# Summing the last two blocks of a prefix-sum kernel on VectorE with two input streams and an accumulator

## The chip, the cores and the metric

One core of a Trainium2 chip. The metric is the device time of one execution in microseconds (us); most executions of a kernel agree within 0.3%. The engines are named as in the profile: PE = TensorE, DVE = VectorE, ACT = ScalarE, POOL = GpSimd, SP = SyncE.

## The reference

```python
B, H, W = 4, 4224, 4224          # x: float32, 285 MB
ps = np.cumsum(np.cumsum(x, axis=1), axis=2)
diag = np.diagonal(ps, axis1=1, axis2=2)
return np.cumsum(diag, axis=1).astype(np.float32)
```

Output i of a batch is a cumulative sum, along the diagonal, of the sums of all x[r, c] with r and c up to i. So every element is read once, and what counts is a sum for each row (left of the diagonal) and for each column (above it).

## The kernel before

The input streams through three strip buffers; GpSimd issues the loads, which convert float32 to bf16. ScalarE and VectorE sum rows, TensorE sums columns. What follows is the end of the last batch, the only part that the change touches. The last 128 rows come as four blocks of 32 rows, each laid out as 128 partitions (4 per row) of 1024 columns. Blocks 0 and half of 1 are folded on TensorE, the rest are summed.

```python
def act_sum(acc, src):                      # ScalarE: copy with accumulator
    w = src.shape[-1]
    dump = dumpool.tile([P, 2176], BF16, name="dump")
    nc.scalar.activation(out=dump[:, :w], in_=src, func=ACT.Copy, accum_out=acc)

def row_sums(acc, src):                     # VectorE: reduction
    nc.vector.reduce_sum(out=acc, in_=src, axis=AX.X)
# ... (the stream, parts of the tail)
bcut = 640                                  # block 3 is loaded in two pieces
for sb, c0, c1 in ((0, 0, CB), (1, 0, CB), (2, 0, CB), (3, 0, bcut), (3, bcut, CB)):
    nc.gpsimd.dma_start(out=part_b[:, sb, c0:c1], in_=...)
# ...
act_sum(bsum[:, 0:1], part_b[:, 1, c1a:])
nc.scalar.copy(out=by, in_=by_ps)
weigh(arows[:, 0:1], weights, 0, fins[:1], start=True)   # fp32 matmuls, [128,1] x [128,n]
weigh(arows[:, 1:2], weights, P, fins[:1])
# ... (arows, dtot, bsum 0 and ones_col into fin_m and fin_e)
finish(fin_a, 0, M0)                        # VectorE: yl = fin + c12
act_sum(bsum[:, 1:2], part_b[:, 2, : CB // 2])
row_sums(bsum[:, 2:3], part_b[:, 2, CB // 2 :])
for k in (1, 2):
    weigh(bsum[:, k : k + 1], weights4, M0 + 2 * R, fins)
esum = last.tile([P, 4], FP32, name="esum")
for k, (c0, cm, c1) in enumerate(((0, 320, bcut), (bcut, bcut + 128, CB))):
    act_sum(esum[:, 2 * k : 2 * k + 1], part_b[:, 3, c0:cm])
    row_sums(esum[:, 2 * k + 1 : 2 * k + 2], part_b[:, 3, cm:c1])
for k in range(4):
    weigh(esum[:, k : k + 1], weights4, E0, fins)
finish(fin_m, M0, E0)
# ... store of 352 values, finish(fin_e), store of 32 values
```

## Time and profile before

| | us |
|---|---|
| time, median of the first 3 runs | 670.04 (669.3 to 670.96) |
| time, median of 6 runs with those of the comparison | 669.36 (668.34 to 670.96) |
| span of the profiled execution | 666.5 |
| landing of block 1, block 2, block 3 first piece, final piece | 660.83, 662.12, 662.91, 663.38 |
| final add (VectorE's addition of the last 32 values) | 664.36 |
| final add behind the final landing | 0.97 |

The landings are from the trace's semaphore records: the time at which the last of the 16 DMA engines reports. I call the last row the gap. (The prediction has 0.98 for it, from rounded times.) The prediction shows the profile lines.

### The profile page before, as it was taken

The numbers are of one execution on the slowest core, as the hardware profiler recorded it, in microseconds if no ns is written. First come the engines' busy times: TensorE is split into PE (matmuls) and PEld (weight loads), VectorE is DVE, ScalarE is ACT, GpSimd is POOL, SyncE is SP. The second block draws the span as 40 slices with busy tenths as digits, with TensorE's granted clock in tenths as the row PEclk, the third lists the DMA queues.
The fourth block names the chain that finished last, engine by engine and source line by source line (L and its number), as shares of the span: only waits on it lengthen the run. The fifth ranks groups of instructions, "written<-read, shape, count | busy, mean of one in ns | idle before, by whom it ended". The sixth has DMA issues, their size and how long they took to land.

```text
span 666.5 us, 2923 instructions
## 1 busy us (share of the span) xinstructions
PE 214.0 (32%) x1011; PEld 99.1 (15%) x1011; DVE 336.1 (50%) x378; ACT 140.6 (21%) x228; POOL 28.0 (4%) x61
## 2 busy tenths in 40 slices
PE   0081522403117153240321633504032264250427
PEld 0030211101003021010110311202011122120104
DVE  3033617366924351745883515265498241635687
ACT  0001120406300103040630020304063002030436
POOL 5000000000000000000000000000000000001000
PEclk9995857656558585675655957656575586666758
DMA  9999999999999999999999999999999999999998
GB/s 203 219 219 219 218 220 218 218 216 204 218 220 218 219 216 219 218 219 219 210 213 220 219 219 214 218 216 218 219 219 218 210 220 220 213 214 219 218 209 154
DMA packets 7673, 143.27 MB, mean 215 GB/s; under 512 B 702, under 2 KB 1002, under 8 KB 2154
## 3 DMA queue, kind: packets, MB, share of 16 engines
q0 software_dynamic: 7296, 142.47, 99.8%
q1 hardware_dynamic: 362, 0.61, 0.3%
q8 instruction: 8, 0.13, 0.1%
q14 instruction: 7, 0.06, 0.0%
HBM read 285.47 MB, written 0.07 MB: 428 GB/s over the span
## 4 chain that ended last, share of the span: by engine, by line
another core or an unknown queue 38%; DVE 24%; PE 21%; DMA 13%; issue 4%; ACT 0%; POOL 0%; DVEq 0%; ACTq 0%; POOLq 0%
PE d L214 21%; DVE acc L240 16%; DMA strip<-in_x_dram 13%; DVE mu L243 6%; ACT dump L235 0%; DVE pu L240 0%; DVE c L243 0%; POOL strip L395 0%; DVE acc L329 0%; DVE acc L326 0%; PE carry_ps L214 0%; DVE rows L354 0%; DVEq L243 0%; DVE rows L363 0%
## 5 line engine op out<-in xcount | busy, mean ns | idle before, releaser
L243 DVE SCALAR_TENSOR_TENSOR mu<-strip,um 128x768 bf16<-128x768 bf16 (+1 forms) x129 | 110.7, 908 | 308.6 <-DMA strip<-in_x_dram 218.0
L214 PE MATMUL d<-strip,sel 128*11 128x384 bf16 x603 | 138.5, 403 | 334.2 <-DMA strip<-in_x_dram 334.2
L235 ACT ACTIVATE dump<-strip 128x416 bf16<-128x416 bf16 (+9 forms) x113 | 128.7, 1139 | 522.5 <-DMA strip<-in_x_dram 519.7
L240 DVE TENSOR_REDUCE acc<-strip 128x6 f32<-128x4608 bf16 (+6 forms) x23 | 195.9, 8518 | 0.0
L214 PEld LDWEIGHTS <-sel 128*11 128x11 bf16 x849 | 85.9, 101 | 514.6 <-issue 476.4
L214 PE MATMUL d<-mu,sel 128*11 128x384 bf16 x243 | 58.6, 348 | 68.2 <-DVE mu L243 68.2
L76 POOL DMA_DIRECT2D strip<-in_x_dram x24 | 16.4, 686 | 554.9 <-DVE acc L240 415.9
L235 ACT ACTIVATION_READ_ACCUMULATOR dump<-strip 128x1 f32 x113 | 21.0, 186 | 0.0
L243 DVE DVE_READ_ACCUMULATOR mu<-strip,um 128x1 f32 x129 | 10.6, 82 | 0.0
L214 PE MATMUL d<-ident,rows 128*11 128x128 f32 x24 | 5.2, 379 | 16.4 <-DVE rows L363 16.4
L214 PE MATMUL fold<-strip,ident_h 128*128 128x480 bf16 x8 | 3.4, 598 | 7.6 <-DMA strip<-in_x_dram 7.6
L214 PE MATMUL d<-halves,rows 128*11 128x64 f32 x48 | 5.3, 290 | 0.0
L214 PEld LDWEIGHTS d<-ident,rows 128*11 128x11 f32 x24 | 2.5, 119 | 18.2 <-DVE rows L363 17.3
L214 PEld LDWEIGHTS d<-halves,rows 128*11 128x11 f32 x48 | 4.7, 128 | 2.0 <-issue 1.9
L240 DVE TENSOR_REDUCE pu<-d 11x1 f32<-11x384 f32 x4 | 2.2, 546 | 5.0 <-PE d L214 5.0
L214 PE MATMUL fold<-weights,quarter 32*128 32x128 f32 x2 | 0.8, 497 | 11.0 <-POOL quarter L200 11.0
L433 DVE TENSOR_TENSOR_SCAN c<-ones_row,carry,c 11x384 f32<-11x384 f32 x4 | 4.0, 1005 | 0.1
L433 DVE TENSOR_TENSOR_SCAN c<-ones_row,carry,d 11x384 f32<-11x384 f32 x4 | 4.0, 1001 | 0.1
L214 PEld LDWEIGHTS <-ident_h 128*128 128x128 bf16 x20 | 2.2, 113 | 11.0 <-issue 10.9
L406 POOL DMA_DIRECT2D strip<-in_x_dram x5 | 2.7, 557 | 22.2 <-DMA strip<-in_x_dram 22.2
L240 DVE TENSOR_REDUCE parts<-strip 128x3 f32<-128x3072 bf16 x1 | 3.3, 3348 | 0.0
L221 DVE COPY weights<-fold 128x128 f32<-128x128 f32 x1 | 0.3, 291 | 5.4 <-PE fold L214 5.4
(102 smaller groups left out, 44.6 us busy)
## 6 DMA issues: line engine op xcount, KB each, us to landing
strip<-in_x_dram POOLq DMA_DIRECT2D x19, 6336.0 KB, 69.6
strip<-in_x_dram POOLq DMA_DIRECT2D x5, 3168.0 KB, 55.4
strip<-in_x_dram POOLq DMA_DIRECT2D x1, 1080.0 KB, 45.6
strip<-in_x_dram POOLq DMA_DIRECT2D x1, 768.0 KB, 48.6
strip<-in_x_dram POOLq DMA_DIRECT2D x3, 256.0 KB, 49.9
head<-in_x_dram SPq DMA_DIRECT2D x1, 528.0 KB, 3.7
strip<-in_x_dram POOLq DMA_DIRECT2D x1, 160.0 KB, 43.5
strip<-in_x_dram POOLq DMA_DIRECT2D x1, 96.0 KB, 28.6
```

The source lines that it names most:

```text
L76: nc.gpsimd.dma_start(out=o, in_=x[b, r0 : r0 + f * P, :].rearrange("(p f) w -> p f w", f=f))
L214: nc.tensor.matmul(o, lhsT=lhsT, rhs=rhs, start=start, stop=False, skip_group_check=True)
L221: nc.vector.tensor_copy(out=weights4, in_=w4_ps)
L235: nc.scalar.activation(out=dump[:, :w], in_=src, func=ACT.Copy, accum_out=acc)
L240: nc.vector.reduce_sum(out=acc, in_=src, axis=AX.X)
L243: nc.vector.scalar_tensor_tensor(out=o, in0=i, scalar=1.0, in1=m, op0=ALU.mult, op1=ALU.mult, accum_out=acc,)
L406: nc.gpsimd.dma_start(out=part_b[:, sb, c0:c1], in_=x[b, r0 : r0 + R, :TB].rearrange("r (k c) -> r k c", k=4)[:, :, c0:c1],)
L433: nc.vector.tensor_tensor_scan(out=c12[:, i, :], data0=ones_row, data1=src, initial=carry[:, i : i + 1], op0=ALU.mult, op1=ALU.add,)
```

## The change

Its intent: halve VectorE's work per column by feeding the two halves of a row as two input streams and letting the accumulator add up the result; and take the final piece off ScalarE, so that one engine sums it alone and TensorE has three sums to weigh instead of four. The final piece shrinks from 384 to 256 columns.

```diff
+    def pair_sum(acc, src):
+        w = src.shape[-1] // 2
+        pair = dumpool.tile([P, 512], FP32, name="pair")
+        nc.vector.scalar_tensor_tensor(
+            out=pair[:, :w], in0=src[:, :w], scalar=1.0, in1=src[:, w:],
+            op0=ALU.mult, op1=ALU.add, accum_out=acc,
+        )
 ...
-            bcut = 640
+            bcut = 768
 ...
-        act_sum(bsum[:, 1:2], part_b[:, 2, : CB // 2])
-        row_sums(bsum[:, 2:3], part_b[:, 2, CB // 2 :])
+        act_sum(bsum[:, 1:2], part_b[:, 2, :448])
+        pair_sum(bsum[:, 2:3], part_b[:, 2, 448:])
 ...
-        esum = last.tile([P, 4], FP32, name="esum")
-        for k, (c0, cm, c1) in enumerate(((0, 320, bcut), (bcut, bcut + 128, CB))):
-            act_sum(esum[:, 2 * k : 2 * k + 1], part_b[:, 3, c0:cm])
-            row_sums(esum[:, 2 * k + 1 : 2 * k + 2], part_b[:, 3, cm:c1])
-        for k in range(4):
+        esum = last.tile([P, 3], FP32, name="esum")
+        act_sum(esum[:, 0:1], part_b[:, 3, :320])
+        pair_sum(esum[:, 1:2], part_b[:, 3, 320:bcut])
+        pair_sum(esum[:, 2:3], part_b[:, 3, bcut:])
+        for k in (1, 0, 2):
             weigh(esum[:, k : k + 1], weights4, E0, fins)
```

(The call of pair_sum is printed on fewer lines than in the file.)

More of the change, by code (lines that the diff above doesn't have):

```diff
@@ L240, in row_sums @@
         nc.vector.reduce_sum(out=acc, in_=src, axis=AX.X)
+    def pair_sum(acc, src):
+        w = src.shape[-1] // 2
+        pair = dumpool.tile([P, 512], FP32, name="pair")
+        nc.vector.scalar_tensor_tensor(
+            out=pair[:, :w],
+            in0=src[:, :w],
+            scalar=1.0,
+            in1=src[:, w:],
+            op0=ALU.mult,
+            op1=ALU.add,
+            accum_out=acc,
+        )
     def masked(o, i, m, acc):
```

## The prediction

> **What bounds the kernel now.** I read the page's table of slices first, then the issue list (part 6), then the chain that ended last, then the timeline of VectorE, ScalarE and TensorE over the last microseconds.
>
> ```profile
> DMA  9999999999999999999999999999999999999998
> GB/s 203 219 219 219 218 220 218 218 216 204 218 220 218 219 216 219 218 219 219 210 213 220 219 219 214 218 216 218 219 219 218 210 220 220 213 214 219 218 209 154
> HBM read 285.47 MB, written 0.07 MB: 428 GB/s over the span
> ```
>
> The DMA engines are full in every slice but the last. The kernel reads 285 MB once, at 428 GB/s, and that sets about 663 of the 666.5 us. The change alters no byte of this. All it can move is what is left when the last bytes land, so I need landing times.
>
> ```profile
> strip<-in_x_dram POOLq DMA_DIRECT2D x1, 160.0 KB, 43.5
> strip<-in_x_dram POOLq DMA_DIRECT2D x1, 96.0 KB, 28.6
> 619.39 0.53 POOL L406 DMA_DIRECT2D strip<-in_x_dram  x1 [7.30 <-DMA strip<-in_x_dram]
> 634.80 0.53 POOL L406 DMA_DIRECT2D strip<-in_x_dram  x1 [14.88 <-DMA strip<-in_x_dram]
> ```
>
> The first two lines are issues with KB and us from issue to landing, the other two are the same issues in GpSimd's timeline. So the first piece of the last block (640 of 1024 columns) lands at 619.39 + 43.5 = 662.9, the second (384 columns) at 634.80 + 28.6 = 663.4. The trace's semaphore records put the landings of the second-to-last block and of these two at 662.12, 662.91 and 663.38. One DMA engine is last each time: the others deliver the final piece by 662.94.
>
> ```profile
> 662.34 0.66 DVE L240 TENSOR_REDUCE bsum<-strip 128x1 f32<-128x512 bf16 x1
> 662.93 0.89 DVE L240 TENSOR_REDUCE esum<-strip 128x1 f32<-128x320 bf16 x2
> 662.20 0.63 ACT L235 ACTIVATE dump<-strip 128x512 bf16<-128x512 bf16 x1 [0.41 <-DMA strip<-in_x_dram]
> 662.99 0.47 ACT L235 ACTIVATE dump<-strip 128x320 bf16<-128x320 bf16 x1
> 663.59 0.31 ACT L235 ACTIVATE dump<-strip 128x128 bf16<-128x128 bf16 x1
> 663.80 0.19 ACT L235 ACTIVATION_READ_ACCUMULATOR dump<-strip 128x1 f32 x1
> 664.04 0.28 PE L214 MATMUL fin_e<-weights,esum 128*1 128x32 f32 x4 [0.16 <-ACT dump L235]
> 664.36 0.18 DVE L477 TENSOR_TENSOR yl<-fin_e,c 1x32 f32<-1x32 f32 x1 [0.38 <-PE fin_e L214]
> ```
>
> The reader is to see who is last. ScalarE takes block 3's 320 columns 0.08 us after their landing (662.91 to 662.99), then the 128 columns of the final piece only at 663.59, 0.21 after that piece landed, because it was busy. Its accumulator read ends at 663.99; TensorE starts the last four matmuls 0.05 later; VectorE adds at 664.36. VectorE's own two reductions are done by 663.82, 0.17 before ScalarE. So the tail after the last landing is ScalarE's second small piece, and the chain says the same:
>
> ```profile
> 663.57 0.02 issue
> 663.59 0.31 ACT dump L235
> 663.90 0.10 ACTq L552
> 664.00 0.04 issue
> 664.04 0.29 PE fin_e L214 x4
> 664.33 0.02 issue
> 664.36 0.18 DVE yl L477
> ```
>
> From the landing at 663.38 to the final add is 0.98 us; that is the whole prize. From the add to the end of the span another 2.15 us pass (the add, the store of 32 values, its landing, the close), which the change doesn't touch.
>
> **What the Trainium skill says.** "VectorE: DVE Perf Modes", section "The perf-mode tier table", gives tensor_reduce one element per cycle at 0.96 GHz, in any type. The trace agrees: 13348 ns for 12672 columns is 1.05 ns a column. No page gives the rate of scalar_tensor_tensor with an accumulator; the trace does, below. The same page, section "Two Vector instructions with no wait between them", says that an op that also writes out its accumulator is two instructions; the trace has a DVE_READ_ACCUMULATOR of 82 ns behind each. "ScalarE: Activation LUTs", section "What ACT_TABLE_LOAD costs", gives an activation with immediates 186 ns + 0.833 ns a column; the trace has 309, 470 and 629 ns for 128, 320 and 512, the same slope and 17 ns more. "DMA: Bandwidth & Descriptors", section "Specifications", wants at least 512 B a transfer for full rate. The new final piece writes 256 bf16 values a row, just 512 B. In the trace the slowest engine's packets of 1280 B start 0.10 us apart and those of 768 B 0.06: proportional to bytes, so I expect 0.04 at 512 B and no loss.
>
> **The change part by part.**
>
> *Cost of a pair sum.* The existing masked products are the same instruction: 278 ns for 128 columns, 555 for 384, 955 for 768, or 143 ns + 1.06 ns a column (two input columns per step). They write bf16 and the new one fp32; I assume the same rate, since the fp32 one in the carry part takes 535 for 384. The accumulator read overlaps and ends 0.01 after. So 288 steps: 448 ns, 224: 380, 128: 278. Replaced are reductions of 512, 320 and 256 columns at 664, 484 and 419 ns. VectorE's tail falls from 1.57 us to 1.11, not to half, as the fixed part is paid again, and for more columns than before (576 + 448 + 256).
>
> *A wait that it adds.* All three pair sums write one scratch tile from a pool of one buffer, and the built program shows that the second and third wait for VectorE's own semaphore. Where the trace has such a self-wait (the two scans of the carries), the next instruction starts 0.04 after the end of the former, where unwaited ones overlap by 0.07. So pair sums cost their full length plus 0.05.
>
> *The landings.* 128 columns move from the final piece to the one before. On the slowest engine the 384 columns take 8 x 0.06 = 0.48 us, so 128 are 0.16: the first piece lands at 662.91 + 0.16 = 663.07, the final one still at 663.38.
>
> *The new tail.* VectorE: block 2's pair starts at 662.34 as now, done at 662.80. Block 3's first pair starts at 663.07 + 0.02 = 663.09, done at 663.48; with the self-wait the final pair starts at 663.52 (its data has been there since 663.38) and is done at 663.81. ScalarE: block 2's 448 columns end sooner (about 662.91 instead of 662.96); its 320 columns wait for the landing, 663.07 + 0.08 = 663.15, and are read out 0.57 later, at 663.72. TensorE now weighs the sums in the order VectorE, ScalarE, VectorE; the last is ready at 663.81, plus 0.05 to 0.15 of release (0.05 behind ScalarE, 0.15 in the carry part behind VectorE): 663.86 to 663.96. Only two matmuls then follow instead of four, 0.06 less, so the final add starts 0.26 after: 664.12 to 664.22, against 664.36. The middle add on VectorE (0.23) runs from 663.78 to 664.01, beside the matmuls, and the store of the first 352 values issues at 664.03 to 664.26, just ahead of the second.
>
> Sum, from the final landing at 663.38 to the final add: before, 0.21 until ScalarE is free, 0.40 for its piece and readout, 0.05 of release, 0.32 for four matmuls: 0.98. After, 0.14 until the self-wait is over, 0.29 for the last pair, 0.05 to 0.15 of release, 0.26 for two matmuls: 0.74 to 0.84. Net gain 0.14 to 0.24 us, about 0.2 us, or 0.03% of 670.
>
> **The rivals.**
>
> *The landing bounds it.* If the slowest engine's last bytes came later than 663.38 (one engine is already 0.45 behind the rest), the final pair would start with the landing and not the self-wait, and the gain would follow the DMA, not the sums. For it: the lag. Against: bytes and queue order are unchanged. A few tenths either way.
>
> *The self-wait and the fixed costs eat the gain.* If the fp32 scratch write ran at half rate, the last two pairs would take 0.23 and 0.13 longer, the final add would fall at about 664.5, and the kernel would be 0.2 us slower. The fp32 product in the carry part speaks against it, though one of its inputs is in PSUM.
>
> *Bigger than I think.* Were the whole 0.98 us between the last landing and the final add removed, which nothing can do, the time would be 669.1. So even that is 0.15%.
>
> *Nothing to see.* The three runs of before spread over 669.3 to 670.96, 1.66 us, eight times the gain. The reading of 285 MB varies by more than the change gives. This I hold most likely.
>
> **Range and chances.** The middle of the runs of before is 670.04, the profiled execution 668.22, and the mean of the four 669.6; I take 669.8 as the level and subtract 0.2: 669.6. The range is the scatter of a median of three runs (about 0.6 either way from the spread shown), doubled because the level of before is itself uncertain: 668.4 to 670.9. A step of 2% is 13.4 us. No part of the change reaches the 663 us of streaming, and the tail behind it is 3.1 us long in all. So within 2% gets nearly everything.
>
> **What would show it right or wrong.** Right: all slices but the last as before; the pair sums at about 450, 380 and 280 ns with an 82 ns read each; the last pair's start 0.04 behind the former's end rather than at its landing; ScalarE's last piece of 320 columns done before the final pair; the final add some 0.7 to 0.85 us after the last landing instead of 0.98. Wrong: pair sums at 2 ns a step, a final piece whose 512 B packets take over 0.06 each, or SyncE's second store held up behind the first. A change of the time by over 2 us would mean that something in the streaming moved, which I see no cause for.

## The result, and the profile after

The changed kernel: 669.33 us, median of 6 runs (668.42 to 669.68), against 669.36 (668.34 to 670.96) of the kernel before, all six runs. The ratio is 0.9995, with a 95% interval of 0.9981 to 1.0009: the same. Ratios here are the mean time of one kernel's runs over that of the other's of the same rounds, so not quite the ratio of the medians quoted.

The profiled execution shows what lies under it. First the two issues of the last block from the page (KB each, us to landing), which the new cut turned from 160 and 96 KB into these:

```profile
strip<-in_x_dram POOLq DMA_DIRECT2D x1, 192.0 KB, 43.7
strip<-in_x_dram POOLq DMA_DIRECT2D x1, 64.0 KB, 28.6
```

The final piece takes as long from issue to landing as before, although it is a third smaller; I read this as waiting in the queue behind the same bytes. By the semaphore records the two pieces land at 663.42 and 663.75. Next VectorE's timeline of the changed kernel (start, duration, in us):

```profile
662.71 0.44 DVE L246 SCALAR_TENSOR_TENSOR pair<-strip 128x288 f32<-128x288 bf16 x1
...
663.51 0.39 DVE L246 SCALAR_TENSOR_TENSOR pair<-strip 128x224 f32<-128x224 bf16 x1 [0.36 <-DMA strip<-in_x_dram]
663.83 0.08 DVE L246 DVE_READ_ACCUMULATOR pair<-strip 128x1 f32 x1
663.95 0.29 DVE L246 SCALAR_TENSOR_TENSOR pair<-strip 128x128 f32<-128x128 bf16 x1
...
664.16 0.24 DVE L491 TENSOR_TENSOR yl<-fin_m,c 1x96 f32<-1x96 f32 x1
664.56 0.18 DVE L491 TENSOR_TENSOR yl<-fin_e,c 1x32 f32<-1x32 f32 x1 [0.15 <-PE fin_e L214]
```

The final piece landed at 663.75, but its pair sum starts at 663.95: 0.04 behind the end of the former's accumulator read (663.91). That is the self-wait. ScalarE's last piece is over earlier, from ScalarE's timeline of the changed kernel:

```profile
663.50 0.47 ACT L235 ACTIVATE dump<-strip 128x320 bf16<-128x320 bf16 x1 [0.26 <-DMA strip<-in_x_dram]
663.88 0.19 ACT L235 ACTIVATION_READ_ACCUMULATOR dump<-strip 128x1 f32 x1
```

It ends at 664.07, the last pair's accumulator read at 664.24, the final add starts at 664.56: a gap of 0.80 instead of 0.97. The gain of 0.17 us is there, in one profile of the changed kernel. The span is nevertheless 0.2 us longer (666.7), because in this execution the final landing came 0.37 us later than in the profile of before. The rest from final add to end is 2.15 us in both.

So far the account closes: a real 0.17 us, drowned in the scatter of the landing. The experiments show that it is not the whole story.

### The profile page after: what moved, and what is told of

Its sections match the earlier page's. It is cut to its first block, busy times and chain, and to the rows that moved or that the text cites. A ratio compares the mean times of both kernels' runs of the same rounds, so it can differ in the third digit from the quotient of the medians.

```text
span 666.7 us, 2921 instructions
## 1 busy us (share of the span) xinstructions
PE 215.4 (32%) x1009; PEld 99.4 (15%) x1009; DVE 335.7 (50%) x381; ACT 140.2 (21%) x226; POOL 28.0 (4%) x61
## 4 chain that ended last, share of the span: by engine, by line
another core or an unknown queue 39%; DVE 24%; PE 21%; DMA 12%; issue 4%; POOL 0%; DVEq 0%; POOLq 0%
PE d L214 21%; DVE acc L240 16%; DMA strip<-in_x_dram 12%; DVE mu L257 6%; POOL strip L420 0%; DVE pu L240 0%; DVE c L257 0%; POOL strip L409 0%; DVE acc L343 0%; DVE acc L340 0%; PE carry_ps L214 0%; DVE rows L368 0%; DVEq L257 0%; PE fin_e L214 0%
## 5 line engine op out<-in xcount | busy, mean ns | idle before, releaser
L235 ACT ACTIVATE dump<-strip 128x416 bf16<-128x416 bf16 (+8 forms) x112 | 128.3, 1146 | 523.0 <-DMA strip<-in_x_dram 520.3
```

## The experiments

Twelve kernels ran. All but one compute the right sums; the exception is named. Gaps are worked out from the records as above. "Edit" is against the changed kernel unless said otherwise.

**Both kernels again.** No edit.

> The kernel before, looked at again to see how well the tail repeats: final add 0.98 us after the final landing, within 0.03; the landing itself may move by 1 us.

> The changed kernel, looked at again: final add 0.81 us after the final landing, within 0.03; the landing itself may move by 1 us.

Measured: before 0.96, as expected. The changed kernel 1.37, far off 0.81, with the same instructions. What differed is in TensorE's timeline of this second look; its first two rows here took 0.81 and 0.33 us in the first look:

```profile
661.75 1.44 PE L214 MATMUL fin_a<-weights,arows 128*1 128x256 f32 x4
662.99 0.52 PE L214 MATMUL fin_m<-weights,arows 128*1 128x96 f32 x2
...
664.82 0.34 PE L214 MATMUL fin_e<-weights,esum 128*1 128x32 f32 x6
```

And the chain that ended last (start, duration, what) has no sum of block 3 in it, only TensorE from the landing of block 1 on:

```profile
661.82 1.37 PE fin_a L214 x4
663.19 0.32 PE fin_m L214 x2
...
664.87 0.07 PE fin_m L214 x2
...
664.96 0.41 DVE yl L491 x2
```

TensorE is the bound of this tail. The cause is the granted clock. The windows view (a stretch, its length, then busy us and instruction count by engine, granted clock, DMA share, GB/s), cut at the clock records, for the second look:

```profile
657.27:660.69 3.42, 1.75 (x19) 1.19 (x18) 2.85 (x6) 2.23 (x6) 0.00 (x0) 1.00 1.12 209
660.69:664.10 3.41, 2.78 (x18) 1.70 (x19) 1.00 (x5) 2.15 (x8) 0.00 (x0) 0.50 0.57 96
```

and for the first look at the changed kernel:

```profile
656.33:659.75 3.42, 2.00 (x18) 1.25 (x16) 2.70 (x6) 2.21 (x5) 0.00 (x0) 1.00 1.09 206
659.75:663.16 3.41, 2.53 (x34) 1.98 (x35) 1.74 (x6) 2.40 (x7) 0.00 (x0) 1.00 0.88 155
```

The clock changes in steps of 3.41 us. In the second look one such step at half clock (0.50) lies over the last matmuls. Of the 14 profiles, 7 have such a step over the matmuls behind the landing of block 1. In all 7 TensorE was busy 1.44 to 1.75 us of the 3.41 us before that step; in the 7 without it, 1.93 to 2.38. What separates them, as far as these lines show, is where the steps fall against TensorE's sparse stretch ahead of block 1. The same sorting holds when the whole of all 14 traces is cut into these steps. Of 720 steps at full clock, the 279 in which TensorE was busy 1.887 us or less were followed by half clock, and the 441 in which it was busy 1.894 us or more by full clock. At half clock, where the same matmuls take longer, the border is higher and less sharp: 1573 steps with 2.72 us or less were followed by half clock, 273 with 2.61 us or more by full clock. All this is a sorting after the fact, by busy times whose ends are modelled, and not an experiment: no run set out to change how busy TensorE is in that stretch. The Trainium skill, "TensorE: Matmul & The Clock Gate", section "Part 1: The HAM clock gate", fits it: it describes a clock that is halved or full depending on how busy the array was in a free-running window of 3413 ns.

The next five looks were meant to take the change apart by the gap. All five fell into the halved clock, so their gaps answer another question than the one asked.

**Three scratch tiles (no self-wait).**

```diff
-        pair = dumpool.tile([P, 512], FP32, name="pair")
+        pairs.append(0)
+        pair = dumpool.tile([P, 288], FP32, name=f"pair{len(pairs)}")
```

> The changed kernel with one scratch tile for each pair sum, so that no pair sum waits for the one before. My theory (tail after the last landing, self-wait counts): the first pair of the last block starts 0.02 us behind its landing instead of 0.09, the last pair starts at the final landing or when the first is through, and the final add starts about 0.69 us after the final landing instead of 0.81. Rival (the landing alone sets the end, the self-wait is hidden): 0.81 stays.

Measured: gap 1.47, half clock; by the gap, neither theory. VectorE's timeline still shows the self-wait, since all data had landed when the sums began. Without it:

```profile
663.47 0.43 DVE L249 SCALAR_TENSOR_TENSOR pair<-strip 128x288 f32<-128x288 bf16 x1
...
663.84 0.37 DVE L249 SCALAR_TENSOR_TENSOR pair<-strip 128x224 f32<-128x224 bf16 x1
...
664.16 0.27 DVE L249 SCALAR_TENSOR_TENSOR pair<-strip 128x128 f32<-128x128 bf16 x1
```

With it, in the second look at the changed kernel:

```profile
663.57 0.44 DVE L246 SCALAR_TENSOR_TENSOR pair<-strip 128x288 f32<-128x288 bf16 x1
...
664.05 0.39 DVE L246 SCALAR_TENSOR_TENSOR pair<-strip 128x224 f32<-128x224 bf16 x1
...
664.48 0.29 DVE L246 SCALAR_TENSOR_TENSOR pair<-strip 128x128 f32<-128x128 bf16 x1
```

From start to start, 0.37 and 0.32 against 0.48 and 0.43: the shared scratch tile costs 0.11 us a pair, though at half clock nothing of it reached the final add.

**Old order of the last matmuls.** `for k in range(3)`.

> The changed kernel, but TensorE weighs the sums in the order ScalarE's, VectorE's, VectorE's. My theory: the last pair ends last either way (0.17 us after ScalarE's readout), two matmuls fit in that time, so the final add stays at 0.81 us after the final landing (0.79 to 0.84). Rival (the order is what gained): 0.87 or more, the two extra matmuls of 0.06.

Measured: gap 1.50, half clock. The order stays untested.

**Cut back at 640.** `bcut = 640`.

> The changed kernel with the cut of the last block back at 640: pair sums of 320 and 384 columns (160 and 192 steps). My theory: the first pair is done 0.07 us before the final landing, so the self-wait is hidden; the last pair starts 0.02 to 0.09 behind the landing and takes 0.36; final add 0.70 to 0.76 us after the final landing, better than 0.81. Rival (a smaller final piece is the better one): 0.85 or more, as the final piece has 64 steps more.

Measured: gap 1.29, half clock. The cut stays undecided. The pair sums of 160 and 192 steps took 0.33 and 0.36 us (326 and 358 ns), 0.01 over the prediction's formula.

**Reductions in place of pair sums.** `row_sums` for all three `pair_sum` calls.

> The changed kernel with plain reductions (576, 448 and 256 columns) in place of the pair sums, all cuts as in the change. My theory: the reduction of 448 columns takes 0.60 us from 0.02 behind its landing, the final one starts 0.22 behind the final landing; final add 0.95 to 1.0 us after it, so the pair sums are worth about 0.17 and the cuts alone nothing. Rival (the cuts and VectorE taking the final piece are what gained): 0.85 or less.

Measured: gap 1.63, half clock. This one look had another bound: its chain runs through VectorE.

```profile
663.06 0.41 DVE yl L491
...
664.13 0.86 DVE esum L240 x2
...
665.04 0.23 PE fin_e L214 x2
```

VectorE adds the first 256 values before its sums, and TensorE delivers those late at half clock. Block 2 had landed at 662.40, but its sum starts only at 663.40, behind that addition, so the slow sums then stick out.

**The kernel before without ScalarE's final piece.** Against the kernel before: the act_sum of 128 columns of the final piece dropped, row_sums over all 384, three sums to weigh.

> The kernel before with one change: VectorE alone reduces the final 384 columns, ScalarE's piece of 128 is gone. My theory: the first reduction is through 0.04 us before the final landing, the last starts 0.02 behind it and takes 0.54, then 0.05 and two matmuls 0.26: final add 0.87 us after the final landing instead of 0.98. Rival (the plain reduction is too slow for it): 0.98 or more.

Measured: gap 1.58, half clock. Not decided.

What these looks do show together: if TensorE is the bound, the final add depends on nothing but when block 1 lands and when the half-clock step ends, and each us of half clock that lies behind the landing of block 1 costs half a us. With L the landing of block 1, E the end of the step and A the final add:

| half-clock look | E - L | A - L | 3.92 + (E - L - 2.82) / 2 |
|---|---|---|---|
| changed kernel again | 2.82 | 3.92 | (anchor) |
| three scratch tiles | 3.03 | 4.02 | 4.02 |
| old order | 3.11 | 4.06 | 4.06 |
| cut 640 | 2.58 | 3.82 | 3.80 |
| kernel before, no ScalarE piece | 3.25 | 4.12 | 4.14 |
| pairs in the stream (below) | 3.21 | 4.10 | 4.12 |
| reductions | 2.61 | 4.19 | 3.82 |

Six of seven kernels, with pair sums, reductions, either cut and either order, lie on one line within 0.02, with one look each. At half clock how block 3 is summed is worth nothing, unless VectorE is as slow as with the plain reductions at the new cuts. The kernel before itself was never caught at half clock; the row without ScalarE's piece is the nearest to it. And since all four looks that were to separate the parts of the change fell into half clock, no run here shows how the 0.17 us at full clock divide among the pair sums, the cut, ScalarE's dropped piece and the order of the matmuls.

**A known extra on the path.**

```diff
+        for _ in range(15):
+            pair_sum(esum[:, 2:3], part_b[:, 3, bcut:])
         for k in (1, 0, 2):
```

> The changed kernel with the last pair sum done 15 more times, each waiting for the one before: a known extra of 15 x 0.33 = 4.95 us (0.278 for 128 steps, 0.01 for the accumulator read, 0.04 for the self-wait). My theory (what lies behind the last landing is on the path one for one, so the 0.17 us saved are real and drown in the scatter): the time rises by 4.9 us, ratio about 1.0074. Rival (the end hangs on something else, such as the close or a straggling transfer, so that a tail saving is worth nothing): the rise is clearly under 4.9 us, in the extreme 0.

Measured: 673.66 us (5 runs) against 668.58 (9 runs), ratio 1.0081, interval 1.0068 to 1.0094, which holds 1.0074. In its profile the last extra pair starts 5.01 us after the regular one of the final piece (668.71 and 663.70), and the gap is 5.85, that is 0.80 + 5.01 + 0.04. The 0.04 belong to the clock, which is full up to 668.33 and half from there on, so over the last two matmuls: from the end of the last pair's accumulator read to the final add it takes 0.36 here and 0.31 in the first look. Taken off, this leaves the changed kernel's 0.80 a second time. From its timeline of TensorE, the matmuls behind the last pair, with the idle time before them:

```profile
669.06 0.27 PE L214 MATMUL fin_e<-weights,esum 128*1 128x32 f32 x2 [4.97 <-DVE pair L246]
```

The tail is on the path one for one. A saving there is worth its full size, as long as VectorE is what TensorE waits for.

**The final piece summed but not weighed.** `for k in (1, 0)`. Wrong; it passed the comparison nevertheless, whose tolerance is too wide to notice 256 columns of the last 32 outputs.

> Wrong on purpose: the sum of the final 256 columns is computed but not weighed in, so TensorE doesn't wait for it. My theory: ScalarE's 320 columns become the last, 0.65 us behind the landing of the first piece plus 0.05 and two matmuls 0.26: the final add at about 0.63 us after the final landing instead of 0.81, a gain of 0.18 and no more, although a whole sum is gone. Rival (VectorE's last pair alone is the tail): the final add at 0.5 us or less.

Measured: gap 0.61 at full clock; 0.63 was expected and the rival's 0.5 is out. ScalarE's readout ended at 664.71, 0.31 before the final add, as expected. But the chain names VectorE:

```profile
664.59 0.30 DVE pair L246 x2
664.89 0.31 DVE yl L491 x2
```

Its queue still held the unweighed pair and the middle add right up to the final one, so ScalarE and VectorE end together here, and the 0.61 does not single out ScalarE. Not waiting for the last sum, while VectorE still computes it, is worth only 0.19 us.

**Pair sums in the stream too.** Each strip's reduction replaced by one pair sum per row block, rotating over three scratch tiles.

```diff
-            row_sums(acc[:, :, 1], strip[:, :, ws:hi])
+            for q in range(f):
+                stream_sum(acc[:, q, 1:2], strip[:, q, ws:hi])   # as pair_sum, tile from mup
```

> The changed kernel with every row sum of the stream done by pair sums too (one per row block instead of one reduction per strip). VectorE's busy time falls from 336 us to about 250. My theory (the stream is bound by the DMA engines): the time stays within 0.2% of the kernel before. Rival (buffers freed earlier let transfers start earlier): faster by 1% or more, and fuller DMA slices.

Measured: 670.04 us (5 runs) against 668.58, ratio 1.002, interval 1.0006 to 1.0034. From the page, busy time by engine and the DMA slices, with 335.7 us for VectorE in the changed kernel:

```profile
PE 214.9 (32%) x1009; PEld 100.0 (15%) x1009; DVE 246.8 (37%) x615; ACT 140.2 (21%) x226; POOL 28.0 (4%) x61
...
DMA  9999999999999999999999999999999999999997
```

89 us of VectorE's work gone, and not faster: it was not the bound. That it is 0.06 to 0.34% slower is not explained; I have no line that shows it.

**The best split of the tail.** Three scratch tiles as above and `bcut = 704`.

> The changed kernel with a scratch tile for each pair sum and the last block cut at 704 (pairs of 192 and 160 steps). My theory: the two landings are 0.40 us apart, the last pair starts 0.02 behind the final landing, final add about 0.65 us after it. The time against the kernel before: 0.3 us less, 0.05%, which five rounds can't tell from nothing: verdict same. Rival (the tail is worth more than the profile shows): a ratio below 0.998.

Measured: 668.76 us (6 runs) against 669.14 (11 runs), ratio 0.9996, interval 0.9984 to 1.0009: the same. Gap 0.67 at full clock, 0.65 expected. Its first pair of block 3 starts 0.03 behind the landing (663.71 to 663.74), where the changed kernel's needs 0.09 to 0.10, and its last pair starts 0.03 behind the final landing (664.11 to 664.14). From VectorE's timeline:

```profile
663.74 0.36 DVE L249 SCALAR_TENSOR_TENSOR pair<-strip 128x192 f32<-128x192 bf16 x1 [0.22 <-DMA strip<-in_x_dram]
664.14 0.33 DVE L249 SCALAR_TENSOR_TENSOR pair<-strip 128x160 f32<-128x160 bf16 x1
```

In the changed kernel the landing is waited for by an instruction of its own ahead of the pair, in its chain this one, which the trace of the best split does not have:

```profile
663.45 0.02 DVEq L246
```

**TensorE's last matmuls in bf16.** On top of the best split: `arows`, `dtot`, `bsum`, `esum`, `by`, `ones_col` and the weights as bf16 tiles.

```diff
-        arows = last.tile([P, 2], FP32, name="arows")
+        arows = last.tile([P, 2], BF16, name="arows")
-        weigh(arows[:, 0:1], weights, 0, fins[:1], start=True)
+        weigh(arows[:, 0:1], weights_h, 0, fins[:1], start=True)
# ... (likewise dtot, bsum, esum, by, ones_col; weights4 becomes weights4_h)
```

> The version with three scratch tiles and the cut at 704, with the row sums, the weights and the folded block that TensorE multiplies at the end held in bf16 instead of fp32 (the input is rounded to bf16 on loading anyway, so the result should stay correct). Seven of the thirteen profiles so far show the granted clock at 0.5 for 3.41 us over the last matmuls, and in those the final add came 1.29 to 1.63 us after the final landing instead of 0.61 to 0.97. My theory: there TensorE's fp32 matmuls are the bound and the sums are hidden. With cheaper matmuls the final add comes at about 0.56 us after the final landing at full clock, and at no more than 0.75 if the clock is halved again; VectorE's wait for the first 256 values before its pair sums is gone or under 1 us. Rival (the halved clock only coincides, and something else is late in those runs): 1.29 or more if the clock is halved. The time: 0.4 us less than before at full clock, about 0.9 at half, so a ratio near 0.999, which five rounds may not tell from 1.

Measured: 668.01 us (5 runs, 667.86 to 669.52) against 669.64 (9 runs), ratio 0.9976, interval 0.9963 to 0.999. The interval leaves out 1: it is the only version that is faster clear of noise. That it passed the comparison says little of its accuracy, as the run with the last piece unweighed passed too. In its profile the clock is full over the matmuls, so it does not test the theory at half clock, and that rival stays open. From TensorE's timeline:

```profile
662.75 0.33 PE L217 MATMUL fin_a<-weights_hh,arows 128*1 128x256 bf16 x2
...
665.06 0.55 PE L217 MATMUL fin_e<-weights_h,esum 128*1 128x32 bf16 x3 [0.32 <-DVE pair L254]
```

The fin_a matmuls that took 0.81 us take 0.33, and TensorE idles where it was packed. The gap is 0.63, not the 0.56 expected. The difference of the means of all these runs, 1.3 us (1.6 by the ratio), is more than the 0.34 that the gap explains at full clock and the roughly 0.9 expected at half; the interval's near end, 0.1% or 0.7 us, would fit a mixture of both. How much of it is the tail is not settled by one profile. The profiled execution was the slowest of the five (669.52), with its final landing at 665.02.

## Why the prediction was right

**The bound.** DMA slices, bytes and 428 GB/s are unchanged in the profile after. Time: 669.33 against 669.6 predicted, in the range, within 2%. How near the time came is luck: the kernel before scatters over 2.6 us, and the ratio's interval (0.19% less to 0.09% more) neither shows nor refutes the predicted 0.03%. (The range, 0.6 doubled about 669.6, should end at 670.8 and not at 670.9.)

**The pair sums.** Predicted 448, 380 and 278 ns; measured 436, 392 and 293, plus accumulator reads of 79 on average. The fp32 scratch costs no half rate, so that rival falls.

**The landings.** Predicted 0.31 us between the two pieces of block 3; measured 0.33. The 512-byte packets follow each other 0.04 us apart, as expected.

**The self-wait.** Predicted 0.04 behind the former's end: measured exactly that. Missed was its second effect. The first pair of block 3 waits for a landing and for VectorE itself, and starts 0.09 after the landing, where 0.02 was predicted. With scratch tiles of their own it is 0.03.

**The gap.** Predicted 0.74 to 0.84; measured 0.80 in the first look, a gain of 0.17 where 0.14 to 0.24 stood. The place inside the range is in part luck. Its width stood for a release of 0.05 to 0.15 behind VectorE. From the last readout to the final add it took 0.31, which is the low end (0.05 + 0.26), so 0.74 should have come. The other 0.06 are mostly the late start of block 3's first pair, which was not foreseen.

**Where it was incomplete.** The prediction took TensorE for a follower in every execution: "Only two matmuls then follow instead of four". In the second look at the changed kernel the gap was 1.37, with the sums hidden behind TensorE at half clock. The rivals named landings, self-wait and scatter, not the clock, though the page of before printed it falling to half in many slices. The scatter that "nothing to see" leaned on has at least two parts: the final landing moved from 663.38 to 665.02 over the 14 profiles, and the gap from 0.80 to 1.37 for the same kernel. The gain is 0.17 us at full clock; at half clock it is about nothing, by the line through six kernels.

## What to carry to other kernels

If a transfer that never pauses sets 99% of the time, first measure what is left between the last landing and the end: that is the most a change of the tail can give, here 0.97 us of 670. Measure such a change by the interval from the last landing to the last dependent instruction, in more than one profile, because TensorE's granted clock over those few us can differ from one execution to the next. Give each of several small sums its own scratch tile.

## What the Trainium skill lacked or had wrong

- "TensorE: Matmul & The Clock Gate", Part 1, gives the window and the two states and says of idle windows that they lead to half clock, and of busy ones that they lead to full. It gives no share for a window that is part busy, such as these. In these 14 traces a full-clock window with 1.887 us or less of 3.41 was followed by half clock (279 of 279) and one with 1.894 or more by full clock (441 of 441). It also says not to trust single clock events on trn2; here the matmuls agree with them (four fin_a matmuls: 0.81 us at full, 1.44 at half; from their start to that of the next matmuls 0.65 and 1.24).
- "VectorE: DVE Perf Modes" has no row for scalar_tensor_tensor with an accumulator: here 293 ns for 128 steps, 392 for 224, 436 for 288, 955 for 768, and 79 to 82 for the accumulator read. (The prediction's "No page gives the rate" holds for the form with an accumulator; elsewhere the skill has a general rate for ops with two sources.)
- The same page says, in the section "The DRAIN you can't avoid", that a semaphore after each of a chain of copies costs nothing extra. That does not carry over to pair sums: here a wait on VectorE's own semaphore cost 0.11 us a pair (starts 0.48 and 0.43 apart against 0.37 and 0.32), and a second wait on one instruction moved its start from 0.03 to 0.09 behind a landing.
- No page that I read says what a half-clock step does to a short tail: here it moved the final add of one kernel from 0.80 to 1.37 us behind the last landing.
